# A decoder layer on one core: the first norm rebuilt, the late gates and the seams around the feed-forward reordered

## The chip, the core and the metric

The kernel runs on one core of one Trainium2 chip. It is written for the five engines TensorE (PE), VectorE (DVE), ScalarE (ACT), GpSimd (POOL) and SyncE (SP). Nearly all data transfers (DMAs) are issued on SP, in one list. The metric is the device time of one execution, in microseconds (us); of several executions the median is given.

## What is computed

One layer of a hybrid decoder on 1024 tokens of width 1024, in float32:

```
u = rms_norm(x, g_mix);  z = u @ w_in          # columns shared by all branches
y_nsa = sparse attention (compressed, selected top 8 blocks, window 512), 16 heads
y_rnn = gelu(gate) * rg_lru(causal_conv(z_rnn))
y_x   = cross attention of 4 heads into 256 memory tokens
h = x + (sum of sigmoid(gate_b) * y_b) @ w_o
v = rms_norm(h, g_mlp)
h = h + square(relu(v @ w_up)) @ w_down        # hidden width 4096
out = rms_norm(h, g_final)
```

## The kernel before

**Products.** A float32 product is made of three matmuls of split operands (`mm3`, L80 in the trace): every operand has a hi part, copied by ACT in a narrower type (`split`, L219), and a lo part, the difference, which DVE (L220) or POOL makes. Names ending in h and l, or beginning with whi and wlo, are such parts. Accumulators are PSUM tiles of 128x512: psg, pst, pss, pso.

**Order.** The program is written for a framework that puts each engine's instructions in a list of its own. Every engine runs its list in order, and SP issues transfers in the order of its list; an instruction whose input or buffer is not ready holds back all that stand behind it. A transfer into a buffer of a pool waits until the buffer's last user is done.

**First norm.** `norm_transposed` (L257 to 272) takes 128 tokens: ACT squares and sums (L208, L211), POOL multiplies the second half of the row by the gain (L261), DVE scales (L262, L263), PE transposes eight blocks into two pss tiles, ACT and DVE split them into `uh` and `ul` (L271, L272). The gain lies in SBUF as 128 equal rows. This runs for all eight tiles, and then the projections follow. One weight chunk of 128 columns (`load_split`: raw load wraw, whi, wlo) is used for two halves of 512 tokens: `z_half` is 8 times `mm3`, 24 matmuls, and ends with a copy out of PSUM (zkv for the first four chunks). `weights` splits the next chunk of `plan` while one is in use.

**Early stage and mix.** A `Weave` interleaves several generators on PE by their costs: first the two compressions, one query group, the cross queries and the token values, then attention, recurrence and merge gates up to about 1385 us. In the second one the lo parts of weights are on POOL (L237).

**Late gates and W_o.** For the last two gate chunks (c = 6, 7) and both token halves, PE makes a half, ACT takes tanh (gm, L1005), DVE adds the attention parts (yn2, ymerge), multiplies and adds the recurrence (L1006 to 1008), and SP stores y_d. After each token half `load_wo` loads and splits W_o's half (woh, wol), lo parts on POOL. `out_tile(j)` then loads y_d of row j in four pieces yr, splits them (yh, yl), makes 48 matmuls in two halves, adds the residual, and norms with gmb; `out_forms` transposes the row into the operands B11, B21, B22 and the sums vr.

**Feed-forward.** Both products use seven products of half blocks instead of eight. The up projection has steps (p, s), p = 0 to 15, with s in the order 1, 6, 2, 5, 7, 3, 4 and 12 matmuls each; T1 to T4 are split sums of the normed rows (two pieces each), ura and urb raw weights, uf their split combinations. `finish` combines the products (u, v, c on DVE), squares them, and POOL makes sums as1 to as4. Of each p seven tiles go to `act_d`. The down projection has steps (s, p) in the order s, then p. `fetch` loads one tile araw from act_d and, for s = 1, the first two of four w_down tiles of p (wd, wdf, wdu); `operands` splits them (df) and for s = 1 replaces one weight by a difference (L1289). Four fetches run ahead. The last four steps run together (AT_ONCE).

## Time and profile before

| what | us |
|---|---|
| median of 3 runs | 2174.86 |
| lowest and highest run | 2170.16, 2176.45 |
| profiled execution | 2167.23 |
| its span, first to last instruction | 2165.4 |
| PE busy in it | 2004.4 |
| mean granted clock of PE, share of full | 0.973 |

The profile is of one execution. Busy times are sums over an engine's instructions. A row of a timeline gives the start, the duration, the engine, the source line, the operation with its output and input, how often in a row, and in brackets how long the engine had been idle and what ended that. In a table of windows a matmul that overlaps the next counts until the next begins, so PE cannot be busier than the window. PEclk is the share of its full clock that PE was granted; 1.00 is 2.4 GHz and 0.50 is 1.2 GHz.

### The profile page before, as it was taken

To read this page: it belongs to the slowest core of one execution; us is meant where nothing else is said; L and a number is where in the kernel's file an instruction comes from. 1 tells how busy PE (TensorE), PEld (TensorE's weight loads), DVE (VectorE), ACT (ScalarE), POOL (GpSimd) and SP (SyncE) were. 2 spreads that over 40 slices of the span, in tenths; PEclk is the share of its full clock that TensorE was granted. 3 is DMA by queue.
4 is the path that set the end of the run, shared out by engine and by line. 5 is a ranking of instruction groups with operands and counts; after the bars stand their busy time and mean duration, and the time that the engine had idled before them with its cause. 6 is when DMAs were issued, how large, how long until landed. Compare 5 with 4: busy or idle time off the path is not lost. (4 is left out here: it accounts for less than half of the span.)

```text
span 2165.4 us, 30202 instructions
## 1 busy us (share of the span) xinstructions
PE 2004.4 (93%) x10276; PEld 1673.8 (77%) x10276; DVE 1466.3 (68%) x3215; ACT 1137.8 (53%) x2237; POOL 656.4 (30%) x587
## 2 busy tenths in 40 slices
PE   6988999999998999998999989799899997999997
PEld 5877877888887887777878778677688885888776
DVE  6244386686777777677877767755776675797564
ACT  5234366776667675676677657543322221444353
POOL 2011020333422433243432331412677764010210
PEclk9998999999999999999999999899999999999999
DMA  5466345411441112433123442542444446834433
GB/s 188 139 182 171 105 120 151 130 60 44 107 127 40 59 51 80 129 104 97 56 64 98 137 138 77 184 152 88 146 147 155 156 160 215 305 110 143 141 94 125
DMA packets 160147, 269.36 MB, mean 124 GB/s; under 512 B 19193, under 2 KB 71161, under 8 KB 159993
## 3 DMA queue, kind: packets, MB, share of 16 engines
q1 hardware_dynamic: 159992, 267.44, 39.9%
q8 instruction: 81, 1.33, 0.3%
q14 instruction: 74, 0.60, 0.1%
HBM read 181.39 MB, written 85.98 MB: 123 GB/s over the span
## 5 line engine op out<-in xcount | busy, mean ns | idle before, releaser
L80 PE MATMUL psg<-uh,whi 128*128 128x512 f32 x928 | 381.5, 411 | 10.7 <-DVE qxl L220 7.7
L80 PE MATMUL psg<-uh,wlo 128*128 128x512 f32 x928 | 370.7, 399 | 0.0
L80 PE MATMUL psg<-ul,whi 128*128 128x512 f32 x928 | 369.8, 398 | 0.0
L597 DVE TENSOR_TENSOR pw<-pst,ph 128x512 fp32r<-128x512 f32 (+1 forms) x352 | 217.4, 622 | 71.0 <-ACT ph L596 69.9
L596 ACT ACTIVATE ph<-pst 128x512 fp32r<-128x512 f32 (+1 forms) x352 | 187.3, 538 | 96.0 <-PE pst L84 94.8
L80 PEld LDWEIGHTS psg<-uh,whi 128*128 128x128 f32 x928 | 177.2, 191 | 38.9 <-DVE qxl L220 7.9
L80 PEld LDWEIGHTS psg<-uh,wlo 128*128 128x128 f32 x928 | 177.1, 191 | 38.8 <-DVE wlo L220 1.1
L80 PEld LDWEIGHTS psg<-ul,whi 128*128 128x128 f32 x928 | 178.0, 192 | 25.3 <-issue 0.4
L237 POOL TENSOR_TENSOR wlo<-wraw,whi 128x512 fp32r<-128x512 f32 x100 | 133.7, 1357 | 186.5 <-ACT whi L235 182.6
L80 PE MATMUL pss<-KA,Q 128*128 128x320 f32 (+5 forms) x416 | 145.1, 352 | 8.5 <-DVE sx L774 3.5
L80 PE MATMUL pss<-KB,Q 128*128 128x320 f32 (+5 forms) x416 | 135.3, 328 | 2.0 <-DMA KB<-q_lo 2.0
L80 PE MATMUL pso<-ph,V 128*128 128x256 f32 (+1 forms) x544 | 130.1, 305 | 6.7 <-DVE fold L604 4.7
L778 ACT ACTIVATE E<-E,sx 128x128 f32<-128x128 f32 (+7 forms) x128 | 98.8, 772 | 52.0 <-DVE sx L774 51.4
L80 PE MATMUL pso<-pw,V 128*128 128x256 f32 (+1 forms) x544 | 124.2, 295 | 0.0
L778 ACT ACTIVATE Ew<-Ew,sx 128x640 f32<-128x640 f32 (+4 forms) x128 | 88.5, 692 | 62.3 <-DVE sx L774 61.8
L84 PE MATMUL pst<-ident,E 128*128 128x128 f32 x576 | 94.6, 280 | 23.1 <-DVE pw L597 15.4
L80 PE MATMUL psg<-df 128*128 128x512 f32 x384 | 100.6, 396 | 14.5 <-ACT df L219 13.4
L80 PEld LDWEIGHTS pso<-ph,V 128*128 128x128 f32 x544 | 96.3, 192 | 21.2 <-DVE fold L604 5.0
L220 DVE TENSOR_TENSOR df<-araw,df 128x512 fp32r<-128x512 f32 x112 | 81.2, 729 | 44.1 <-ACT df L219 43.9
L219 ACT ACTIVATE df<-araw 128x512 fp32r<-128x512 f32 x112 | 68.9, 620 | 73.8 <-DMA araw<-act_d 35.5
L80 PE MATMUL pss<-df 128*128 128x512 f32 x432 | 106.2, 389 | 0.7 <-ACT df L219 0.7
L84 PEld LDWEIGHTS pst<-ident,E 128*128 128x128 f32 x576 | 71.6, 143 | 37.0 <-issue 21.6
(405 smaller groups left out, 5043.3 us busy)
## 6 DMA issues: line engine op xcount, KB each, us to landing
wraw<-in_wz SPq DMA_DIRECT2D x59, 512.0 KB
araw<-act_d SPq DMA_DIRECT2D x112, 256.0 KB
act_d<-as SPq DMA_DIRECT2D x64, 256.0 KB
act_d<-sq SPq DMA_DIRECT2D x48, 256.0 KB
yn_d<-parts SPq DMA_DIRECT2D x64, 128.0 KB
ura<-in_w_up SPq DMA_DIRECT2D x16, 512.0 KB
urb<-in_w_up SPq DMA_DIRECT2D x16, 512.0 KB
wdu<-in_w_down SPq DMA_DIRECT2D x32, 256.0 KB
```

The source lines that it names most:

```text
L80: self.tc.nc.tensor.matmul(out, w, x, start=start, stop=stop, skip_group_check=more)
L84: self.tc.nc.tensor.transpose(out, x, ident)
L219: act.activation(hi, src, AF.Copy)
L220: (lo_eng or dve).tensor_tensor(lo, src, hi, OP.subtract)
L237: pool.tensor_tensor(lo[:, x], raw[:, x], hi[:, x], OP.subtract)
L596: act.activation(ph[:rows, :w], pt[:rows, :w], AF.Copy)
L597: dve.tensor_tensor(pw[:rows, :w], pt[:rows, :w], ph[:rows, :w], OP.subtract)
L778: act.activation(E[:, :nw], E[:, :nw], AF.Exp, bias=sx[:, hh:hh + 1], scale=-1.0, accum_out=sx[:, 2 + hh:3 + hh])
```

## The change

- The first norm: the gain is loaded as a column of 128x8 and multiplied in the two splits. DVE scales the x tile in place. Four token tiles are transposed together, feature row by feature row, pss and pst in turn. The order is: norm and split of tokens 0 to 511, norm of the others, first halves of two projection chunks, split of the others, second halves. Raw weights of those chunks are loaded between the x tiles.
- `weights`: the raw load runs two chunks ahead, the split one; the plan already holds five chunks at the start of the early stage. The two compressions are interleaved after 17 and 3 steps.
- Late gates: for the second token half, tanh goes to a DRAM tile tn_d, and the merge follows after row 0 of W_o, in other buffers. W_o's second half gets its lo parts on DVE.
- Last W_o rows: rows 6 and 7 are interleaved by halves; half of T2 and T1 is split before the last half of row 7. `form` takes ten instead of seven early slots.
- Stores of the up projection are collected and issued when step s = 2 of the next p is reached; for the last p they are issued at the fourth down step. The first four down fetches move ahead of the last p's steps, and the differences of w_down are made for p - 3.
- AT_ONCE is 3.

The diff, cut to its core:

```diff
-            uh = actT(F32R, "uh")
-            ul = actT(F32R, "ul")
+            uh, ul = token_halves("uh", "ul")
...
             def weights(src, shape):
-                if not plan:
+                if not plan and not ready:
                     return load_split(src, shape)
-                if not ready:
-                    ready.append(load_split(*plan.pop(0)))
-                w = ready.pop(0)
+                for n in (1, 2):
+                    if len(ready) < n and plan:
+                        what = plan.pop(0)
+                        ready.append([what[1], load_raw(*what), None])
+                for r in ready:
+                    r[2] = r[2] or load_split(None, r[0], raw=r[1])
+                w = ready.pop(0)[2]
                 if plan:
-                    ready.append(load_split(*plan.pop(0)))
+                    what = plan.pop(0)
+                    ready.append([what[1], load_raw(*what), None])
                 return w
...
+                gmix = e0.tile([P, KC], F32, name="gmix")
+                dma(gmix, A["g_mix"])
+                xts, wrs = [], []
                 for j in range(NQ):
+                    if j in (4, 6):
+                        wrs.append(load_raw(*z_weights(KV_CHUNK + len(wrs))))
                     xt = rw("xn") if j < 6 else e0.tile([P, D], F32, name="xn", bufs=2)
                     dma(xt, A["x"][j * P:(j + 1) * P, :])
                     xts.append(xt)
-                    if j == 0:
-                        dma(gmix, A["g_mix"].unsqueeze(0).broadcast_to([P, D]))
-                for j in range(NQ):
-                    xn = e0.tile([P, D], F32, name="xnj", bufs=3)
-                    norm_transposed(xts[j], xn, (gmix[:, :512], gmix[:, 512:]), tok_dst(uh, ul, j))
...
+                def norm_rows(th):
+                    for j in range(4 * th, 4 * th + 4):
+                        x = xts[j]
+                        r = rms_scale(x, e0.tile([P, D], F32, name="xnj", bufs=3))
+                        dve.tensor_scalar(x, x, r, None, OP.mult)
+
+                def feature_rows(th):
+                    for k in range(KC):
+                        pt = (ps_s, ps_t)[k % 2]()
+                        for j in range(4):
+                            pe.transpose(pt[:, j * P:(j + 1) * P], xts[4 * th + j][:, k * P:(k + 1) * P], ident)
+                        h, l = cols(uh, k, th * 512, 512), cols(ul, k, th * 512, 512)
+                        act.activation(h, pt, AF.Copy, scale=gmix[:, k:k + 1])
+                        dve.scalar_tensor_tensor(l, pt, gmix[:, k:k + 1], h, OP.mult, OP.subtract)
...
+                norm_rows(0)
+                feature_rows(0)
+                norm_rows(1)
+                kv0 = [(0, ch, load_split(*z_weights(KV_CHUNK + ch), raw=wrs[ch]), rw("zkv"))
+                       for ch in range(2)]
...
+                for kv, ch, w, zt in kv0:
+                    kv_half(zt, w, 0)
+                feature_rows(1)
+                for kv, ch, w, zt in kv0:
+                    kv_half(zt, w, 1)
+                    kv_store(kv, ch, zt)
...
+                    for x, n in ((a, 17), (b, 3)):
+                        for _ in range(n):
+                            yield next(x)
...
+            def merge_late(t, yn, n2, c, hf):
+                cs = slice(hf * 512, hf * 512 + 512)
+                dma(yn[:, 1, :], yn_d[0][c, :, cs])
+                dma(n2, yn_d[1][c, :, cs])
+                dma(yn[:, 0, :], yr_d[c, :, cs])
+                dve.tensor_tensor(n2, n2, yn[:, 1, :], OP.add)
+                dve.scalar_tensor_tensor(t, t, 1.0, n2, OP.add, OP.mult)
+                dve.tensor_tensor(t, t, yn[:, 0, :], OP.add)
+                dma(y_d[hf][c], t)
...
-                    yn = st("ymerge", F32, (P, 2, 512))
-                    dma(yn[:, 0, :], yr_d[c, :, cs])
-                    dma(yn[:, 1, :], yn_d[0][c, :, cs])
-                    n2 = half2("yn2")
-                    dma(n2, yn_d[1][c, :, cs])
-
                     def use(cs, ps):
                         t = half("gm")
                         act.activation(t, ps, AF.Tanh, scale=0.5)
-                        dve.tensor_tensor(n2, n2, yn[:, 1, :], OP.add)
-                        dve.scalar_tensor_tensor(t, t, 1.0, n2, OP.add, OP.mult)
-                        dve.tensor_tensor(t, t, yn[:, 0, :], OP.add)
-                        dma(y_d[hf][c], t)
+                        if hf:
+                            dma(tn_d[c, :, cs], t)
+                        else:
+                            merge_late(t, st("ymerge", F32, (P, 2, 512)), half2("yn2"), c, hf)
                     for _ in z_half(late[c - 6], hf, use):
                         pass
-                load_wo(hf)
+                load_wo(hf, (pool, dve)[hf])
...
+                if j == 0:
+                    vr.update((n, ox.tile([P, 4, 512], F32, name="vr" + n)) for n in ("11", "21", "12", "22"))
+                    gmb = ox.tile([P, D], F32, name="gmb")
+                    dma(gmb, A["g_mlp"].unsqueeze(0).broadcast_to([P, D]))
+                for nh in range(2):
+                    out_half(row, nh)
+                if j == 0:
+                    for c in (6, 7):
+                        t = spare("gm1")
+                        dma(t, tn_d[c, :, 512:])
+                        merge_late(t, form("ymerge", F32), spare("yn2"), c, 1)
...
+            rows = [out_rows(NQ - 2)]
+            out_half(rows[0], 0)
+            out_forms(NQ - 3, prev)
+            rows.append(out_rows(NQ - 1, form("h7", F32).rearrange("p a b -> p (a b)")))
+            out_half(rows[1], 0)
+            out_half(rows[0], 1)
+            xa = out_norm(NQ - 2, rows[0])
+            first = (("t2", "22"), ("t1", "12"))
+            for n, src in first:
+                t_form(n, src, slice(0, 256))
+            out_half(rows[1], 1)
+            out_forms(NQ - 2, xa)
+            xb = out_norm(NQ - 1, rows[1])
             run(0, 1)
             finish(0, 1)
-            out_forms(NQ - 1, prev)
+            prep(0, 5)
...
+            out_forms(NQ - 1, xb)
             run(0, 2)
-            for n, src in (("t2", "22"), ("t1", "12"), ("t3", "11"), ("t4", "21")):
-                B[n] = vform("T" + n[1], False)
-                for k in (slice(0, 2), slice(2, 4)):
-                    split(B[n][0][:, k, :], B[n][1][:, k, :], vr[src][:, k, :])
+            for n, src in first:
+                t_form(n, src, slice(256, 512))
+            for n, src in (("t3", "11"), ("t4", "21")):
+                t_form(n, src, slice(0, 512))
...
+            stores = []
+
+            def store_acts():
+                while stores:
+                    i, p, t = stores.pop(0)
+                    dma(act_d[i - 1][p], t)
...
-                    for i, t in ((1, a11), (4, a22), (5, s1), (6, s2), (7, s3)):
-                        dma(act_d[i - 1][p], t)
+                    stores.extend((i, p, t) for i, t in ((1, a11), (4, a22), (5, s1), (6, s2), (7, s3)))
...
+                if s == 2:
+                    store_acts()
+                if p == NP - 1 and s == 1:
+                    while n_f < 4:
+                        fetched[dsteps[n_f]] = fetch(*dsteps[n_f], act_tile)
+                        n_f += 1
...
-                    dve.tensor_tensor(w[1], w[1], w[0], OP.subtract)
+                    for x in ((p - 3,) if p < NP - 1 else range(p - 3, NP)):
+                        if x >= 0:
+                            dve.tensor_tensor(wd[x][0][1], wd[x][0][1], wd[x][0][0], OP.subtract)
...
-            AT_ONCE = 4
-            fetched, ready_, banks, keep_ = {}, {}, {}, {}
-            n_f = n_r = 0
-            n = 0
+            AT_ONCE = 3
...
+                if n == 3:
+                    store_acts()
```

The built order, at three places. First ScalarE (ACT) in the first norm. L208 and L213 are the squares of an x tile, L211 and L216 the roots, L219 and L224 hi parts of weights. Before, around the first weights:

```order
L208 ACTIVATE xnj_291,rms_ss_292<-xn_121 128x1024
L211 ACTIVATE rms_r_294<-rms_r_294 128x1
L271 ACTIVATE uh_95<-pss_253 128x4x128
L271 ACTIVATE uh_97<-pss_260 128x4x128
L219 ACTIVATE whi_326<-wraw_324 128x1024
L271 ACTIVATE uh_95<-pss_277 128x4x128
L271 ACTIVATE uh_97<-pss_284 128x4x128
L219 ACTIVATE whi_386<-wraw_384 128x1024
```

After, the same place:

```order
L224 ACTIVATE whi_247<-wraw_115 128x1024
L213 ACTIVATE xnj_215,rms_ss_216<-xn_117 128x1024
L346 ACTIVATE uh_94<-pss_159,gmix_105 128x512
L346 ACTIVATE uh_94<-pst_166,gmix_105 128x512
L346 ACTIVATE uh_94<-pss_173,gmix_105 128x512
L346 ACTIVATE uh_94<-pst_180,gmix_105 128x512
L346 ACTIVATE uh_95<-pss_187,gmix_105 128x512
L346 ACTIVATE uh_95<-pss_201,gmix_105 128x512
L346 ACTIVATE uh_95<-pst_194,gmix_105 128x512
L216 ACTIVATE rms_r_218<-rms_r_218 128x1
L213 ACTIVATE xnj_223,rms_ss_224<-xn_119 128x1024
L346 ACTIVATE uh_95<-pst_208,gmix_105 128x512
```

The first chunk's hi part now stands before all splits of u, each of which covers 512 tokens of one feature row, and the squares of the later tokens stand among them.

Second VectorE (DVE) at the end of the late gates: L1006 to 1008 (now L1048 to 1050) are the merges, yl the lo parts of row 0, wol those of W_o. Before:

```order
L1007 SCALAR_TENSOR_TENSOR gm_14749<-gm_14749,yn2_14722 128x512
L1008 TENSOR_TENSOR gm_14749<-gm_14749,ymerge_14719 128x512
L1006 TENSOR_TENSOR yn2_14778<-yn2_14778,ymerge_14775 128x512
L1007 SCALAR_TENSOR_TENSOR gm_14805<-gm_14805,yn2_14778 128x512
L1008 TENSOR_TENSOR gm_14805<-gm_14805,ymerge_14775 128x512
L1006 TENSOR_TENSOR yn2_14814<-yn2_14814,ymerge_14811 128x512
L1007 SCALAR_TENSOR_TENSOR gm_14841<-gm_14841,yn2_14814 128x512
L220 TENSOR_TENSOR yl_14893<-yr_14894,yh_14892 128x256
L1008 TENSOR_TENSOR gm_14841<-gm_14841,ymerge_14811 128x512
L220 TENSOR_TENSOR yl_14893<-yr_14898,yh_14892 128x256
L220 TENSOR_TENSOR yl_14893<-yr_14902,yh_14892 128x256
L220 TENSOR_TENSOR yl_14893<-yr_14906,yh_14892 128x256
```

After:

```order
L1048 TENSOR_TENSOR yn2_14724<-yn2_14724,ymerge_14723 128x512
L1049 SCALAR_TENSOR_TENSOR gm_14721<-gm_14721,yn2_14724 128x512
L1050 TENSOR_TENSOR gm_14721<-gm_14721,ymerge_14723 128x512
L225 TENSOR_TENSOR yl_14848<-yr_14849,yh_14847 128x256
L225 TENSOR_TENSOR yl_14848<-yr_14853,yh_14847 128x256
L225 TENSOR_TENSOR wol_14811<-woraw_14808,woh_14810 128x1024
L225 TENSOR_TENSOR wol_14811<-woraw_14814,woh_14810 128x1024
L225 TENSOR_TENSOR wol_14821<-woraw_14818,woh_14820 128x1024
L225 TENSOR_TENSOR wol_14821<-woraw_14824,woh_14820 128x1024
L225 TENSOR_TENSOR yl_14848<-yr_14857,yh_14847 128x256
L225 TENSOR_TENSOR yl_14848<-yr_14861,yh_14847 128x256
```

The merges of the second token half have gone from here, and four wol stand between row 0's second and third lo part.

Third SP, where the down projection's first loads are issued. araw are stored activations, sq and as tiles to be stored. Before, at the end of the last p's stores:

```order
L1274 DMA wdu_18391<-in_w_down 128x512
L1189 DMA act_d_85<-sq_18139 128x512
L1274 DMA wdf_18271<-in_w_down 128x512 x2
L1274 DMA wdf_18295<-in_w_down 128x512
L1189 DMA act_d_85<-as1_18157 128x512
L1189 DMA act_d_85<-as2_18158 128x512
L1189 DMA act_d_85<-as3_18159 128x512
L1196 DMA act_d_85<-sq_18182 128x512
L1197 DMA act_d_85<-as4_18184 128x512
L1279 DMA araw_18188<-act_d_85 128x512
L1279 DMA araw_18194<-act_d_85 128x512
L1279 DMA araw_18200<-act_d_85 128x512
```

After, the first araw loads:

```order
L1202 DMA act_d_85<-as2_18009 128x512
L1357 DMA araw_18036<-act_d_85 128x512
L1357 DMA araw_18042<-act_d_85 128x512
L1357 DMA araw_18048<-act_d_85 128x512
L1352 DMA wdf_18050<-in_w_down 128x512 x2
L1357 DMA araw_18053<-act_d_85 128x512
L1352 DMA wdf_18055<-in_w_down 128x512 x2
L1202 DMA act_d_85<-as3_18010 128x512
L1202 DMA act_d_85<-sq_18032 128x512
L1202 DMA act_d_85<-as4_18034 128x512
```

The loads of the first four steps moved from behind the last p's stores to the middle of those of the p before, with their w_down tiles between them.

## Rows read from the trace of the kernel before

**Rows 1.** The page, its first part: busy us, share, instructions of each engine.
```profile
PE 2004.4 (93%) x10276; PEld 1673.8 (77%) x10276; DVE 1466.3 (68%) x3215; ACT 1137.8 (53%) x2237; POOL 656.4 (30%) x587
```

**Rows 2.** Windows: length, then busy us (instructions) of each engine, PEclk, DMA share, GB/s.
```profile
core 0: us, PE busy (x) PEld busy (x) DVE busy (x) ACT busy (x) POOL busy (x), PEclk, DMA share, GB/s
...
0.00:25.00 25.00, 10.14 (x40) 7.55 (x40) 16.23 (x31) 15.33 (x30) 8.53 (x13) 1.00 0.84 308
...
1394.43:1425.00 30.57, 18.05 (x66) 13.74 (x67) 19.21 (x22) 9.81 (x20) 15.04 (x8) 0.78 0.46 153
...
1506.35:1547.00 40.65, 30.07 (x119) 23.29 (x119) 31.59 (x33) 17.29 (x25) 24.84 (x16) 0.92 0.37 122
1818.90:1850.00 31.10, 16.79 (x57) 12.94 (x58) 20.99 (x31) 7.22 (x13) 5.74 (x4) 0.78 0.85 295
1850.00:1875.00 25.00, 25.00 (x112) 20.69 (x111) 14.89 (x24) 10.39 (x18) 0.00 (x0) 1.00 0.94 322
```

**Rows 3.** Timeline, the start: time, duration, engine, line, operation, [idle before]; ACT, DVE, PE.
```profile
4.45 1.06 ACT L208 ACTIVATE xnj<-xn 128x1024 f32<-128x1024 f32 x1 [2.44 <-DMA xn<-in_x]
...
57.37 0.58 ACT L341 ACTIVATE zkv<-psg 128x512 f32<-128x512 f32 x1
...
9.07 1.53 DVE L263 TENSOR_SCALAR xnj<-xn,rms_r 128x512 f32<-128x512 f32 x1
...
12.24 0.47 DVE L263 TENSOR_SCALAR xnj<-xn,rms_r 128x512 f32<-128x512 f32 x1
...
31.66 0.80 PE L80 MATMUL psg<-uh,whi 128*128 128x512 f32 x1
```

**Rows 4.** Timeline, seam 1, in order: PE, DVE, POOL, SP.
```profile
1384.64 0.40 PE L80 MATMUL psg<-uh,whi 128*128 128x512 f32 x1
...
1394.03 0.40 PE L80 MATMUL psg<-uh,wlo 128*128 128x512 f32 x1
...
1405.63 0.76 PE L80 MATMUL psg<-woh,yh 128*128 128x512 f32 x1 [11.20 <-issue]
...
1390.55 0.69 DVE L1007 SCALAR_TENSOR_TENSOR gm<-gm,yn 128x512 f32<-128x512 f32 x1
...
1395.65 2.71 DVE L1007 SCALAR_TENSOR_TENSOR gm<-gm,yn 128x512 f32<-128x512 f32 x1
...
1392.62 10.68 POOL L220 TENSOR_TENSOR wol<-woraw,woh 128x1024 fp32r<-128x1024 f32 x4 [13.24 <-ACT woh L219]
...
1401.14 0.32 SPq L1009 DMA_DIRECT2D y_d<-gm  x1
```

**Rows 5.** Timeline, seam 2: DVE, then PE.
```profile
1511.91 3.61 DVE L220 TENSOR_TENSOR T2l<-vr,T2h 128x1024 fp32r<-128x1024 f32 x2 [1.12 <-ACT T2h L219]
1515.44 2.35 DVE L220 TENSOR_TENSOR T1l<-vr,T1h 128x1024 fp32r<-128x1024 f32 x2
...
1541.01 0.80 PE L80 MATMUL psg<-B21h,uf 128*128 128x512 f32 x1 [4.78 <-ACT p1s L1163]
```

**Rows 6.** Timeline, seam 3: PE, DVE, PE, ACT, SP.
```profile
1822.96 0.50 PE L80 MATMUL pss<-B22h,uf 128*128 128x512 f32 x1 [4.06 <-DVE v L1173]
...
1818.86 0.69 DVE L1289 TENSOR_TENSOR wdf<-wdf 128x512 f32<-128x512 f32 x1 [7.32 <-DMA wdf<-in_w_down]
...
1840.53 3.31 PE L80 MATMUL psg<-df 128*128 128x512 f32 x6 [10.24 <-ACT df L219]
...
1839.32 0.63 ACT L219 ACTIVATE df<-araw 128x512 fp32r<-128x512 f32 x1 [25.18 <-DMA araw<-act_d]
...
1836.52 5.71 SPq L1279 DMA_DIRECT2D araw<-act_d  x8
```

**Rows 7.** Timeline, early stage: ACT, then PE.
```profile
162.74 1.06 ACT L235 ACTIVATE whi<-wraw 128x1024 fp32r<-128x1024 f32 x1 [14.97 <-DMA wraw<-in_wz]
...
165.06 0.80 PE L80 MATMUL psg<-uh,whi 128*128 128x512 f32 x1 [7.70 <-DVE qxl L220]
```

**Rows 8.** The page, its fifth part: one group, the lo parts on POOL.
```profile
L237 POOL TENSOR_TENSOR wlo<-wraw,whi 128x512 fp32r<-128x512 f32 x100 | 133.7, 1357 | 186.5 <-ACT whi L235 182.6
```

More of the change, by code (lines that the diff above doesn't have):

```diff
@@ L146, in body, with token_halves @@
         w4 = w4_stack.enter_context(tc.tile_pool(name="w4", bufs=1))
[L148 to L149 removed]
+        def token_halves(*names):
+            ts = [[[None, None], [None, None]] for _ in names]
+            for th in range(2):
+                for t, n in zip(ts, names):
+                    for kh in range(2):
+                        t[kh][th] = big.tile([P, 4, 512], F32R, name=n, tag="ut", bufs=8)
+            return ts
         def cols(t, k, c0, w):
@@ L1202, in body, with t_form @@
             load_up(0)
-            for j in range(NQ):
-                xt = out_tile(j)
+            def t_form(n, src, js):
+                if n not in B:
+                    B[n] = vform("T" + n[1], False)
+                w = js.stop - js.start
+                for k in ((slice(0, 4),) if w <= 256 else (slice(0, 2), slice(2, 4))):
+                    split(B[n][0][:, k, js], B[n][1][:, k, js], vr[src][:, k, js])
+            for j in range(NQ - 2):
+                row = out_rows(j)
+                if j == 0:
[9 more added lines that the diff above has]
+                        merge_late(t, form("ymerge", F32), spare("yn2"), c, 1)
+                xt = out_norm(j, row)
                 if prev is not None:
@@ L1238, in act_tile @@
                 return ux.tile([P, 512], F32, name=name, tag="a", bufs=8)
-            LEAD = 6
-            finish(0, 2)
-            todo = steps[2:]
-            at = 2
-            for n, (p, s) in enumerate(todo):
-                while at < len(todo) and at <= n + LEAD:
-                    q, u = todo[at]
-                    load_up(q)
-                    prep(q, u)
-                    at += 1
-                    load_up(q + 1)
-                run(p, s)
-                finish(p, s)
             wd = []
@@ L1282, in fetch @@
                 return araw
+            LEAD = 6
+            finish(0, 2)
+            todo = steps[2:]
+            at = 2
+            dsteps = [(s, p) for s in ORDER_P for p in range(NP)]
+            fetched = {}
+            n_f = 0
+            for n, (p, s) in enumerate(todo):
+                if s == 2:
[4 more added lines that the diff above has]
+                        n_f += 1
+                while at < len(todo) and at <= n + LEAD:
+                    q, u = todo[at]
+                    load_up(q)
+                    prep(q, u)
+                    at += 1
+                    load_up(q + 1)
+                run(p, s)
+                finish(p, s)
             def operands(s, p, araw):
```

98 lines of the change are left out of this document (51 added, 47 removed).

## Prediction

> **What bounds the kernel now.** I read the page's busy times first: TensorE (PE) works 93% of the span [rows 1], so the time is PE's work plus the places where PE stops or is given half its clock. A cost on another engine counts only where PE waits for it. The work itself is untouched: the change removes no matrix product, so the most it can bring is the time that PE loses. Then I read the windows for stretches in which PE is far from 25 busy us in 25 [rows 2], and the timelines of all engines there [rows 3 to 6].
>
> At full clock one 128x512 matmul starts 0.229 us after the one before: 42 of them start from 1384.64 to 1394.03 [rows 4]. I call 24 of them a half (5.5 us) and 12 a step (2.75 us). With that price the windows [rows 2] give the loss of each stretch:
> - Start: the first real matmul is at 31.66 us [rows 3]. The fourth half is copied out of PSUM at 57.37 (ScalarE's zkv row).
> - Seam 1, before the W_o rows: 66 matmuls need 15.1 us and take 30.57. Loss 15.5.
> - Seam 2, before the up projection: 119 matmuls, all counted as full ones, need 27.3 us and take 40.65. Loss at least 13.
> - Seam 3, up to down projection: 57 matmuls need 13.1 us and take 31.10. Loss 18.
>
> The change touches all four. Between them PE is close to full, as in the last window of rows 2, and I expect nothing there.
>
> **Part 1, the first norm.** Before, every tile of 128 tokens is multiplied by the gain on POOL and DVE, and the first product waits for eight such tiles, nearly. Removed: 8 POOL multiplies, the 512 KB gain broadcast, and the DVE multiplies by the gain. Added: eight in-place scalings of 128x1024 on DVE. A 128x512 scaling takes 0.47 us, or 1.53 us beside POOL's multiplies [rows 3], so one costs 0.94 to 3.06; since POOL's eight multiplies are gone I take 0.94. The gain now rides in the two splits, which I price as before. The path to the first matmul is then: x0 is there at 4.45; at the window's 308 GB/s a 512 KB tile takes 1.7 us, so x3 is there at about 9.6; square 1.06, root and reciprocal some 0.6, scaling 0.94, transposes and first split some 2 (estimates): first matmul at 14 to 15. The first half runs at the pace of the DVE splits and partly at half clock, to about 22. The second chunk's weight split stands behind the squares of tokens 512 to 1023 on ScalarE, so its half ends near 31. The splits of the later tokens stand behind that half's copy on ScalarE; two more halves end near 44. That is 13 us ahead of 57.4; I take **12**. High end 15, if the second chunk does not wait. Low end 8, if the first 24 matmuls all run at half clock (5.5 us more, of which part is already in the sum).
>
> **Part 2, raw weights two chunks ahead.** The idea fits one wait: ScalarE waits 14.97 us for a raw chunk [rows 7]. In the built order of the SP queue, however, those two raw loads stand behind the same query stores as before, and in the attention and recurrence stage the loads stand where they stood: the scheduler had already moved them as early as the two raw buffers allow. I take **0**. The three interleaved steps of the two compressions move a few matmuls past others: 0 as well, -2 to +2 us.
>
> **Part 3, seam 1.** PE stops after the last gate half and is idle 11.20 us [rows 4]. The chain: the four lo parts of W_o's second half run on POOL (10.68 us for four). Beside them DVE's merge operations take 2.71 us instead of 0.69. So the last y_d store that row 0 needs is issued at 1401.14, and the loads of row 0 stand behind it on SP. After the change these four lo parts are on DVE (four at 1.18 to 1.3, by rows 5 about 1.2: 4.7 us), two of the four merges come after row 0, and the first two loads of row 0 stand ahead of that store. The merge of chunk 7 then ends near 1396.5, and row 0 starts there, 9 us earlier. Three losses remain, since DVE runs its list in order. Row 0's lo parts 4 to 7 stand behind the four W_o splits, so PE waits about 3 us after 12 to 24 matmuls. Row 1's last two loads stand on SP behind the stored late merge, which itself comes behind row 0's end on DVE: about 3 us more. And the clock falls again in such gaps, 1 to 2 us. Of 15.5 I take back **8**; 13 if PE finds other matmuls in the gaps, 4 if each gap also costs a stretch at half clock.
>
> **Part 4, seam 2.** The splits T2, T1, T3, T4 take DVE 3.61 + 3 x 2.35 = 10.7 us [rows 5]. Half of T2 and T1 is now done before the last row's second half, so some 3 us leave the stretch between the last rows and the first products with T4. The 4.78 us stall at 1541.01 hangs on a POOL chain behind the weight load that follows T4; that chain keeps its order and only starts earlier. I take **3**. Zero if the earlier halves just delay the evacuation of the last row, 7 if the small T2 stalls and the stall at 1541 go too.
> The trace shows that DVE and POOL slow each other: T2l took 3.61 beside POOL, T1l 2.35 without. The Trainium skill (GPSIMD Engine Reference, Specifications) says that the two share their SBUF interfaces when a DVE instruction reads two SBUF inputs. That rule speaks against moving the T halves to where POOL makes the sums of the last rows: by it this term would be 2 and the sum 37.
>
> **Part 5, seam 3.** Two stalls. 4.06 us at 1822.96: a sum v stands on DVE behind a wait of 7.32 us for down weights [rows 6]. 10.24 us at 1840.53: the first operand of the down projection waits for its stored activations, whose loads are issued at 1836.52, behind the last stores. The rest of the 18 is half clock. Now the first four loads and their weights stand on SP ahead of the last sums' stores, the first two operands are split during the last up steps, and the weight differences are spread over the steps. The first down product no longer waits. The sum v still stands behind two weight differences whose loads come only a little earlier than before, so I leave up to 3 us of the first stall and its clock. I take **15**, with ends 7 and 18. What is late next: the fifth operand, whose load follows the last as-sums of POOL. Four steps of 2.75 us cover it with about 2 us to spare.
> Three instead of four steps at the very end, and the removed buffers: 0, within 1 us.
>
> **Sum.** 12 + 0 + 8 + 3 + 15 = 38 us. The profiled execution took 2167.23 us (span 2165.4 and 1.8 around it), so it would be 2129. It lies 7.6 us under the median of the runs, 2174.86; I take the 38 from the median: **2137 us**. All high ends (15, 2, 13, 7, 18: 55) give 2120, all low ends (8, -2, 4, 0, 7: 17) 2158.
>
> **Rivals.**
> 1. *Seam 3 is given back to the DMA.* In the first 16 down steps each needs 3 tiles of 256 KB in 2.75 us, 286 GB/s, and 14 delayed stores come on top: 16.3 MB in 44 us is 369 GB/s. The window after the seam moved 322 GB/s at a DMA share of 0.94 [rows 2]: 50.5 us, 6.5 longer. For it: stores now compete with the loads. Against: four steps are fetched ahead while PE still has 19 us of up steps. It would give 2137 + 6.5 = about 2144.
> The Trainium skill (DMA: Bandwidth & Descriptors, Specifications) gives some 358 GB/s as one core's limit to HBM; by that figure the same 16.3 MB take 45.5 us and this rival costs 1.5 us, 2139. No window of rows 2 comes up to it.
> 2. *The start's gain is small.* DVE and ScalarE run in order, and the second chunk's split could hold PE until all eight tiles are scaled. Then only the gain broadcast and the POOL multiplies are saved, about 3 us instead of 12: 2146. For it: that split stands behind the later squares. Against: the first half needs none of them.
> 3. *Slower: the SP queue blocks.* A raw load two chunks ahead takes the buffer that an earlier chunk's split still reads. If such a load stands at the head of SP, everything behind it waits until POOL's lo part is done (100 of them, 1357 ns each, row in [rows 8]), that is 50 chunks. At 1 us of PE wait each, it costs 50: 2137 + 50 = 2187. It decides from 38/50 = 0.76 us a chunk. For it: POOL already spends 182.6 us waiting for the hi parts, so a split that comes late is nothing rare. Against: the SP order is practically the same, and PE's full windows leave no such waits.
> 4. *The two-ahead load does what its words say*, against the built order. The 14.97 us wait goes, and with it at most PE's gap of 7.70 at 165.06 [rows 7]: 2129.
>
> **How the numbers follow.** Forecast 0.58, rival 1 0.14, rival 2 0.14, rival 4 0.05, rival 3 0.04, and 0.05 that several terms fail together and the time stays within 0.3%. A measurement of this kernel tells about 0.3% (6.5 us) from no change. Faster by more: 0.91; within: 0.05; slower: 0.04. Rivals 1, 2 and 4 lie inside the ends of the sum. The upper end of the range is 2158. The lower one is 2114: all high ends, and 6 of the 7.6 us by which the profiled execution lies under the median. Rival 3 and the failures are outside.
>
> **What would show it.** Right: first 128x512 matmul near 15 us and the fourth copy of zkv near 44; no PE gap over 4 us at the W_o rows, DVE merges at 0.69; no PE gap over 3 us where the up projection ends, and the first df split of ScalarE before the last up step. Wrong: the wait of 14.97 us gone; PE gaps with a DMA named in the first 16 down steps (rival 1); raw weight waits of ScalarE in the middle of the kernel (rival 3); T-splits over 3 us each with POOL busy beside them.

## The result

The changed kernel takes 2138.36 us in the median of four runs (2136.38 to 2142.09), the kernel before 2174.13 beside it. The ratio is 0.9839, with a 95% interval of 0.9819 to 0.9859: faster by 35.8 us. The prediction was 2137.0, with a range from 2114 to 2158. Measured once more later, it took 2136.13 beside a median of 2168.45 for the kernel before, ratio 0.9846 (0.9827 to 0.9864): 32.3 us. The profiled execution took 2138.6 us, its span is 2136.8 against 2165.4.

I divided both traces at the same PE instructions. Stage lengths in us (the time from the one instruction to the next):

| stage | before | after | change |
|---|---|---|---|
| start to first matmul of a projection | 31.66 | 14.16 | -17.5 |
| to first memory projection | 50.05 | 54.28 | +4.2 |
| to first key product of attention (early stage) | 191.80 | 189.34 | -2.5 |
| to last late-gate matmul (mix) | 1120.52 | 1129.63 | +9.1 |
| to first W_o matmul of row 0 | 11.60 | 0.23 | -11.4 |
| W_o rows | 96.27 | 99.05 | +2.8 |
| to first matmul with T4 | 26.00 | 26.48 | +0.5 |
| up projection | 302.00 | 300.50 | -1.5 |
| to first down matmul | 10.63 | 0.23 | -10.4 |
| down projection and tail | 324.87 | 322.90 | -2.0 |

These sum to -28.6, the difference of the two spans. The medians differ by 35.8, since the profiled execution of before lay 7 us under its median. The +4.2 belongs to the -17.5 above it (the first matmul now runs before the later tokens are normed), the +2.8 to the -11.4. The one stage that lost with nothing gained beside it, the mix, is taken up in the experiments.

**The page after**, first part, the answer to [rows 1]:

```profile
PE 2000.6 (94%) x10276; PEld 1670.9 (78%) x10276; DVE 1463.2 (68%) x3211; ACT 1135.0 (53%) x2234; POOL 631.6 (30%) x573
```

PE has the same 10276 instructions and 3.8 us less busy time: 24.8 of the 28.6 us were idle time of PE. **Windows of after**, the answer to [rows 2] (start, seam 1, seam 2, seam 3, and twice the down projection behind it), columns as there:

```profile
0.00:25.00 25.00, 14.97 (x78) 12.49 (x79) 15.53 (x36) 21.10 (x42) 1.51 (x7) 1.00 0.78 296
...
1387.80:1418.40 30.60, 26.95 (x110) 21.45 (x109) 18.48 (x30) 12.76 (x27) 6.00 (x4) 0.89 0.70 230
1491.00:1532.00 41.00, 32.79 (x123) 25.00 (x123) 32.79 (x32) 16.02 (x24) 24.56 (x16) 0.88 0.38 119
1803.00:1834.00 31.00, 27.20 (x114) 22.30 (x114) 23.69 (x36) 9.34 (x17) 6.23 (x4) 0.94 0.90 316
1815.00:1840.00 25.00, 25.00 (x112) 20.68 (x111) 17.85 (x27) 10.68 (x19) 5.30 (x4) 1.00 0.95 336
1834.00:1859.00 25.00, 25.00 (x112) 20.68 (x111) 18.41 (x30) 12.36 (x23) 0.00 (x0) 1.00 0.95 339
```

Seam 1 now holds 110 instructions of PE where it held 66, seam 3 114 where it held 57. Seam 2 holds 123 where it held 119: it hardly moved.

**The start**, timeline of after, the answer to [rows 3] (ACT, DVE, PE):

```profile
8.97 0.75 DVE L338 TENSOR_SCALAR xn<-xn,rms_r 128x1024 f32<-128x1024 f32 x1
...
14.16 0.63 PE L80 MATMUL psg<-uh,whi 128*128 128x512 f32 x1
...
22.43 0.64 ACT L359 ACTIVATE zkv<-psg 128x512 f32<-128x512 f32 x1
...
29.15 0.60 ACT L359 ACTIVATE zkv<-psg 128x512 f32<-128x512 f32 x1 [3.58 <-PE psg L80]
...
44.10 0.58 ACT L359 ACTIVATE zkv<-psg 128x512 f32<-128x512 f32 x1
```

The four copies of zkv are the ends of four halves; the fourth stands at 44.10 instead of 57.37.

**Seam 1**, timeline of after, the answer to [rows 4] (PE, DVE, POOL, SP):

```profile
1387.41 0.39 PE L80 MATMUL psg<-uh,wlo 128*128 128x512 f32 x1
1387.64 0.39 PE L80 MATMUL psg<-woh,yh 128*128 128x512 f32 x1
...
1407.09 1.94 PE L84 MATMUL pss<-ident,xres 128*128 128x128 f32 x8 [2.46 <-DVE xres L1131]
1410.02 0.80 PE L80 MATMUL psg<-woh,yh 128*128 128x512 f32 x1 [0.99 <-ACT yh L224]
...
1386.08 2.36 DVE L225 TENSOR_TENSOR wol<-woraw,woh 128x1024 fp32r<-128x1024 f32 x2 [0.52 <-ACT woh L224]
...
1402.63 1.65 DVE L1049 SCALAR_TENSOR_TENSOR gm<-gm,yn 128x512 f32<-128x512 f32 x1
...
1402.12 1.62 POOL L1179 TENSOR_TENSOR urb<-urb 128x512 f32<-128x512 f32 x1
...
1405.58 0.32 SPq L1051 DMA_DIRECT2D y_d<-gm  x1
...
1405.99 0.94 SPq L1108 DMA_DIRECT2D yr<-y_d  x2
```

The 11.20 us gap is gone: row 0 follows the last gate matmul at once. Two W_o lo parts take DVE 2.36 us. What is left is a gap of 2.46 and one of 0.99, 20 us later: the first before the transposes of row 0, whose norm stands on DVE among the late merge, the second at row 1, whose last two loads (yr) are issued right behind the store of that merge (y_d).

**Seam 2**, timeline of after, the answer to [rows 5] (DVE, POOL, PE):

```profile
1474.84 1.32 DVE L225 TENSOR_TENSOR T2l<-vr,T2h 128x1024 fp32r<-128x1024 f32 x1 [1.20 <-ACT T2h L224]
...
1490.93 2.38 DVE L1131 SCALAR_TENSOR_TENSOR xres<-h,rms_r,gmb 128x1024 f32<-128x1024 f32 x1
1493.24 1.76 DVE L225 TENSOR_TENSOR uf<-urb,uf 128x512 fp32r<-128x512 f32 x1
...
1498.47 1.77 DVE L225 TENSOR_TENSOR uf<-ura,uf 128x512 fp32r<-128x512 f32 x1
...
1500.17 2.29 DVE L225 TENSOR_TENSOR T2l<-vr,T2h 128x1024 fp32r<-128x1024 f32 x1
...
1490.97 1.27 POOL L1153 TENSOR_TENSOR vr<-vr,vr 128x512 f32<-128x512 f32 x1 [13.66 <-DVE rms_r L1100]
1492.20 2.26 POOL L1154 TENSOR_TENSOR vr<-vr,vr 128x512 f32<-128x512 f32 x1
...
1526.18 0.50 PE L80 MATMUL psg<-B21h,uf 128*128 128x512 f32 x1 [4.69 <-ACT p1s L1224]
```

The stall of 4.78 us at p1s (the copy of step 1's product, which ScalarE takes out of PSUM) is still 4.69, and these four DVE operations from 1490.93 on, beside POOL, take 1.9 to 2.6 times what they take in the run without POOL beside them, below. T2's first half, moved ahead of the last row, takes 1.32. The same place before, from the last norm on (DVE, then POOL):

```profile
1506.02 1.28 DVE L1076 SCALAR_TENSOR_TENSOR xres<-h,rms_r,gmb 128x1024 f32<-128x1024 f32 x1
...
1507.55 1.45 DVE L220 TENSOR_TENSOR uf<-ura,uf 128x512 fp32r<-128x512 f32 x1 [0.25 <-ACT uf L219]
...
1506.25 2.19 POOL L1098 TENSOR_TENSOR vr<-vr,vr 128x512 f32<-128x512 f32 x1 [8.36 <-DVE vr L1097]
```

**Seam 3**, timeline of after, the answer to [rows 6] (PE, DVE, SP, ACT):

```profile
1806.99 0.80 PE L80 MATMUL pss<-B22h,uf 128*128 128x512 f32 x1 [3.80 <-DVE v L1234]
...
1813.67 0.39 PE L80 MATMUL pss<-T4h,uf 128*128 128x512 f32 x1
1813.90 1.52 PE L80 MATMUL psg<-df 128*128 128x512 f32 x6
...
1803.16 0.69 DVE L1392 TENSOR_TENSOR wdf<-wdf 128x512 f32<-128x512 f32 x1 [1.10 <-DMA wdf<-in_w_down]
...
1806.26 0.68 DVE L1234 TENSOR_TENSOR v<-pss,u 128x512 f32<-128x512 f32 x1
...
1794.86 1.40 SPq L1357 DMA_DIRECT2D araw<-act_d  x3
...
1797.71 0.63 ACT L224 ACTIVATE df<-araw 128x512 fp32r<-128x512 f32 x1 [4.76 <-DMA araw<-act_d]
...
1820.84 0.63 ACT L224 ACTIVATE df<-araw 128x512 fp32r<-128x512 f32 x1 [8.78 <-DMA araw<-act_d]
```

The first activations are loaded at 1794.86 and split at 1797.71, so the first down matmul follows the last up matmul by 0.23 us. The stall on v has only gone from 4.06 to 3.80.

### The profile page after: what moved, and what is told of

The parts are those of the page before. It is cut to its first block, busy times and chain, and to the rows that moved or that the text cites. A ratio compares the mean times of both kernels' runs of the same rounds, so it can differ in the third digit from the quotient of the medians.

```text
span 2136.8 us, 30179 instructions
## 1 busy us (share of the span) xinstructions
PE 2000.6 (94%) x10276; PEld 1670.9 (78%) x10276; DVE 1463.2 (68%) x3211; ACT 1135.0 (53%) x2234; POOL 631.6 (30%) x573
## 4 chain that ended last, share of the span: by engine, by line
PE 60%; DVE 15%; DMA 8%; ACT 6%; issue 6%; POOL 4%; SPq 1%; POOLq 0%; DVEq 0%; ACTq 0%
PE psg L80 29%; PE pss L80 16%; PE pst L80 6%; PE pso L80 5%; PE pst L84 4%; DVE pw L645 2%; DVE W L951 1%; DVE Ew L822 1%; DMA yn<-yn_d 1%; DMA q_hi<-W 1%; DMA wraw<-in_wz 1%; DVE sx L837 1%; DVE E L822 1%; DMA X<-kv_d 1%; DMA q_lo<-W 1%
## 5 line engine op out<-in xcount | busy, mean ns | idle before, releaser
L224 ACT ACTIVATE df<-araw 128x512 fp32r<-128x512 f32 x112 | 69.1, 620 | 68.2 <-DMA araw<-act_d 29.3
```

Source lines behind the costliest of these rows:

```text
L224: act.activation(hi, src, AF.Copy)
```

## The experiments

Each kernel is given with its ratio to the kernel before, timed beside it, whose medians lay between 2168.2 and 2169.1 us.

**The kernel before, once more.** No edit; one profiled run.

> The kernel before once more, for a second trace of it. In its first trace the mix stage, from the first product of queries with keys to the last gate half, took 1120.1 us (273.5 to 1393.6), in the trace of the changed kernel 1129.2 (257.8 to 1387.0). Theory 1 (the first trace was a lucky execution, it lay 7 us under its median): the mix takes 1126 to 1130 here and the span is near 2172. Theory 2 (the change costs the mix 9 us): 1120 again, span near 2166.

It took 2170.36 us, with a span of 2168.6. The same code gave a mix of 1124.42 us where the first trace has 1120.52, between the two theories; the stages around the seams agree within 1.6 us. So a single trace's mix says nothing under some 4 us.

**Part 1 alone**, put on the kernel before.

```diff
-                for j in range(NQ):
-                    xn = e0.tile([P, D], F32, name="xnj", bufs=3)
-                    norm_transposed(xts[j], xn, (gmix[:, :512], gmix[:, 512:]), tok_dst(uh, ul, j))
...
+                norm_rows(0)
+                feature_rows(0)
+                norm_rows(1)
```

> Only the rebuilt first norm, on the kernel before (the gain tile gmb and the sums vr are allocated a row later, which should cost nothing). Theory that the terms add: 13 us off the start stay, 2174 - 13 = 2161. Rival, that later stages are bound by transfers and give the start's gain back: 2168 to 2174, with the mix longer by as much.

2153.56 us, ratio 0.9939 (0.9916 to 0.9962): 14.9 us, and 14.2 in the trace up to the first key product (259.29 against 273.51). Part 1 is worth a little more than the 12 predicted. This kernel also keeps the changed order of the loads around W_o (gmb is loaded a row later, the merges' inputs behind the tanh). Row 0 starts 3.09 us after the last gate matmul, not 11.60, but the rows then take 104.99 instead of 96.27: an earlier start alone brings nothing at seam 1.

**Without part 2.**

```diff
-                for n in (1, 2):
-                    if len(ready) < n and plan:
-                        what = plan.pop(0)
-                        ready.append([what[1], load_raw(*what), None])
...
+                    ready.append(load_split(*plan.pop(0)))
...
-                early.lead(compress_both(), EARLY)
+                early.lead(seq([compress(0, "w_cmp_k1", "w_cmp_k2", "pos_k"),
```

> The changed kernel with the weights one chunk ahead, an empty plan at the start of the early stage and the two compressions one after the other, as before. My theory, that this part is worth 0: 2138, mix 1129. Rival, that the raw loads two ahead cost the mix its 9 us: 2129, mix 1120. Second rival, that the part brings what its words say, the 14.97 us wait: 2142 to 2146.

2136.17 us, ratio 0.9855 (0.9830 to 0.9881): the same time as with it. Part 2 gains nothing that the medians show. In the changed kernel ScalarE's long wait for a raw chunk is still there (ACT), and with it PE's gap:

```profile
146.98 1.06 ACT L245 ACTIVATE whi<-wraw 128x1024 fp32r<-128x1024 f32 x1 [13.50 <-DMA wraw<-in_wz]
...
149.30 0.80 PE L80 MATMUL psg<-uh,whi 128*128 128x512 f32 x1 [6.19 <-DVE qxl L225]
```

**Without part 3** (late merge and W_o lo parts as before).

```diff
-                        if hf:
-                            dma(tn_d[c, :, cs], t)
-                        else:
-                            merge_late(t, st("ymerge", F32, (P, 2, 512)), half2("yn2"), c, hf)
+                        merge_late(t, st("ymerge", F32, (P, 2, 512)), half2("yn2"), c, hf)
...
-                load_wo(hf, (pool, dve)[hf])
+                load_wo(hf, pool)
```

> The changed kernel with the second token half of the late gates merged at once and W_o's second lo parts on POOL, as before. Theory (these two close the first seam, 8.6 us from the last gate half to the end of the W_o rows in the traces): that stretch is 107 to 109 us again instead of 99.3, the time 2138 + 8.6 = 2147. Rival (the earlier allocation order of the loads closes it, not the merge): stretch 99 to 102, time under 2142.

2144.43 us, ratio 0.9899 (0.9872 to 0.9925). Gap and W_o rows take 107.3 us, against 99.3 with part 3: 8.0 us. Merge and lo parts were put back together, so how the 8.0 divide between them is not shown. The timeline (PE, DVE, POOL) has the cause that the prediction gave, four lo parts on POOL and merges of 2.69 beside them:

```profile
1396.50 0.80 PE L80 MATMUL psg<-woh,yl 128*128 128x512 f32 x1 [6.88 <-DVE yl L225]
...
1386.41 2.69 DVE L1049 SCALAR_TENSOR_TENSOR gm<-gm,yn 128x512 f32<-128x512 f32 x1
...
1383.38 10.68 POOL L225 TENSOR_TENSOR wol<-woraw,woh 128x1024 fp32r<-128x1024 f32 x4 [12.93 <-ACT woh L224]
```

**Without part 4** (rows 6 and 7 and the T splits as before).

```diff
-            for j in range(NQ - 2):
+            for j in range(NQ):
...
-            out_half(rows[1], 0)
-            out_half(rows[0], 1)
...
+            for n, src in (("t2", "22"), ("t1", "12"), ("t3", "11"), ("t4", "21")):
```

> The changed kernel with rows 6 and 7 one after the other and T1 to T4 split whole after the last row, as before. My term was 3 us; the traces show the stretch from the last W_o matmul to the first product with T4 at 26.5 us against 26.0 and 27.6 in two traces of before. Theory now (the earlier halves lie beside POOL and cost what they save): rows plus that stretch 125.8 us within 1, time 2138. Rival (the term of 3 is there, hidden by something else): 2141.

2137.18 us, ratio 0.9864 (0.9839 to 0.9889). W_o rows and stretch to T4 take 124.96 us, with part 4 125.53 and 124.36 in two traces. Part 4 is worth 0, not 3.

**Seam 2 without POOL.** The sums vr of rows 6 and 7 and three activation sums (as1 to as3) of p = 0 go from POOL to DVE.

```diff
-                        pool.tensor_tensor(vr["21"][:, :, js], vr["21"][:, :, js], t2, OP.subtract)
+                        eng = dve if j >= 6 else pool
+                        eng.tensor_tensor(vr["21"][:, :, js], vr["21"][:, :, js], t2, OP.subtract)
...
-                    pool.tensor_tensor(s1, a21, a22, OP.add)
+                    eng = dve if p == 0 else pool
+                    eng.tensor_tensor(s1, a21, a22, OP.add)
```

> The changed kernel with POOL's sums for rows 6 and 7 (four) and the as-sums of p = 0 (three) moved to DVE, 7 x 0.69 = 4.8 us more work there. Theory (DVE is slowed beside POOL: 2.29 us for one T2l piece of 1.18, 2.38 for a scaling of 1.28, 1.75 to 1.78 for uf splits of 0.68): pieces at their lone times, the first products with T4 1 to 2 us earlier, the 4.69 us gap at p1s down to 2 to 3, time 2138 - 3 = 2135. Rival (the seam hangs on the weight load after the splits, not on DVE's speed): gaps as they are or longer by the added work, 2138 to 2142.

2132.74 us, ratio 0.9845 (0.9821 to 0.9869). Its timeline (DVE, PE) shows the same operations as in seam 2 of after, at their own price:

```profile
1488.34 1.28 DVE L1131 SCALAR_TENSOR_TENSOR xres<-h,rms_r,gmb 128x1024 f32<-128x1024 f32 x1
1489.53 0.69 DVE L225 TENSOR_TENSOR uf<-urb,uf 128x512 fp32r<-128x512 f32 x1
...
1495.37 1.23 DVE L225 TENSOR_TENSOR T2l<-vr,T2h 128x1024 fp32r<-128x1024 f32 x1
...
1516.78 0.50 PE L80 MATMUL psg<-B21h,uf 128*128 128x512 f32 x1 [1.52 <-ACT p1s L1225]
...
1529.23 0.50 PE L80 MATMUL pss<-B22h,uf 128*128 128x512 f32 x1 [3.98 <-DVE v L1235]
```

2.38, 1.76 and 2.29 became 1.28, 0.69 and 1.23, the stretch to T4 fell from 26.48 to 23.98, the p1s stall from 4.69 to 1.52. A new wait of 3.98 on v came 12 us later. Over all traces with part 4 the stretch is 25.4 to 26.6 us in the six with POOL's sums and 23.9 to 24.0 in the four without them, so POOL beside DVE costs it 1.4 to 2.7 us, even with the sums' own time then on DVE. The kernel without part 4 was not run with these sums on DVE; that they cost just part 4's gain is therefore not shown. For the whole time the intervals do not part this kernel from the changed one.

**Without part 5** (stores at once, no early fetch, differences at s = 1).

```diff
+                    store_acts()
...
-                if s == 2:
-                    store_acts()
-                if p == NP - 1 and s == 1:
-                    while n_f < 4:
...
-                    for x in ((p - 3,) if p < NP - 1 else range(p - 3, NP)):
...
+                    dve.tensor_tensor(w[1], w[1], w[0], OP.subtract)
```

> The changed kernel with the up projection's stores issued at once, the down projection's first fetches after the last up step, and the weight differences made in the step that needs them. Theory (this part alone closes the third seam): 2138 + 13 = 2151, PE gaps of about 4 and 10 us back. Rival (the seam closes because other parts moved the queue): under 2143.

2147.66 us, ratio 0.9911 (0.9883 to 0.9940), 11.5 us more than the kernel without part 2, timed beside it. The three edits were put back together, so their shares are not shown. Its timeline (PE, ACT, SP) is that of before again:

```profile
1820.37 3.31 PE L80 MATMUL psg<-df 128*128 128x512 f32 x6 [9.65 <-ACT df L224]
...
1819.17 0.63 ACT L224 ACTIVATE df<-araw 128x512 fp32r<-128x512 f32 x1 [23.98 <-DMA araw<-act_d]
...
1816.36 5.71 SPq L1359 DMA_DIRECT2D araw<-act_d  x8
```

**The w_down differences on POOL.** A test of the 3.80 us stall that part 5 left.

```diff
-                            dve.tensor_tensor(wd[x][0][1], wd[x][0][1], wd[x][0][0], OP.subtract)
+                            pool.tensor_tensor(wd[x][0][1], wd[x][0][1], wd[x][0][0], OP.subtract)
```

> The changed kernel with the w_down differences on POOL instead of DVE. Theory (the 3.80 us gap that is left at the third seam comes from the sum v, which stands on DVE behind two such differences that wait for their loads): gap 2.5 or less, time 2138 - 1 to -3. Rival (the gap comes from the activation load whose split stands before v as well, landed at 1803.8): gap 3 or more, no change.

2133.68 us, ratio 0.9841 (0.9820 to 0.9862). The stall is gone (PE, then POOL), so it was DVE's queue of differences:

```profile
1802.85 0.50 PE L80 MATMUL pss<-B22h,uf 128*128 128x512 f32 x1 [0.36 <-DVE v L1234]
...
1800.14 1.51 POOL L1392 TENSOR_TENSOR wdf<-wdf 128x512 f32<-128x512 f32 x1 [4.85 <-DMA wdf<-in_w_down]
```

The up projection is 4.8 us shorter; the down projection is 1.7 longer (324.7), but two kernels without this edit have 324.4 as well. Against the changed kernel's 0.9839 and 0.9846 the time is not told apart.

**The changed kernel again.** No edit, as the measure for the next two.

> The changed kernel once more, beside the two below. If the mix stage differs between executions of one kernel (1120.5 and 1124.4 us in two traces of before, 1121 to 1130 in eight kernels whose mix was not touched but for the load order), it is between 1120 and 1130 here too, and all other stages are within 1 us of the first trace: start to first key product 257.8, gates to rows' end 99.3, up stage 300.5, down stage 310.5. Rival (the change itself makes the mix 9 us longer): 1129 or more again.

2136.13 us, ratio 0.9846 (0.9827 to 0.9864). The mix is 1128.85 us, as long as in the first trace of this kernel, which fits either statement on it within 0.2 us; the stretch to T4 is 1.1 us shorter, the other stages agree within 0.5.

**Both edits**, of seam 2 without POOL and of the differences on POOL.

```diff
+                        eng = dve if j >= 6 else pool
...
+                    eng = dve if p == 0 else pool
...
+                            pool.tensor_tensor(wd[x][0][1], wd[x][0][1], wd[x][0][0], OP.subtract)
```

> The changed kernel with POOL's sums for rows 6 and 7 and the as-sums of p = 0 on DVE, and the w_down differences on POOL: both edits at once. If they add (3.8 and 3 us in the traces): 7 us under the changed kernel of this call. If the second is given back in the down stage (312.3 against 310.5 us): 4 to 5.

2131.02 us, ratio 0.9828 (0.9807 to 0.9850). Stretch to T4 and up projection take 318.4 us, against 326.1 (25.35 + 300.73) in the changed kernel timed beside it. Of these 7.7 the medians show 5.1, inside the intervals.

**Both edits, the activation sums left on POOL.** The second of the three lines above is left out.

> As the one before, but the as-sums of p = 0 stay on POOL. In the trace with them on DVE the 4.69 us gap at p1s fell to 1.52 while a new one of 3.98 came at a sum v just behind. If the two only trade places, this kernel is as fast as the one before within 1 us; if moving the as-sums is what helps, it is 2 us slower.

2132.41 us, ratio 0.9832 (0.9816 to 0.9848), the two stages 321.6 us. So of the 7.7 us some 3 hang on the activation sums. No form of the two edits is shown to beat the changed kernel; the two timed beside it lie 5.1 and 3.7 us under it, and by their ratios the two single edits do not lie under it at all.

**Both edits, without part 2**, whose diff stands above. The mix was 1120.5 to 1124.4 us in the four traces without part 2 and 1125.3 to 1130.1 in nine with it.

> The kernel both_fixes (2131.0) without the raw weights two chunks ahead: the plan is filled ahead as before, the compressions stand together as before. Theory that part 2 costs the first norm's mix some 5 us (the stretch from the first key product to the last gate matmul was 1120.5 to 1124.4 in four traces without it, 1125.3 to 1130.1 in those with it): that stretch is 1124.5 or shorter, and the median about 2126, ratio to before about 0.980. Rival, that the stretch's length is only the spread between executions: median about 2131, ratio 0.983 as both_fixes, the stretch anywhere between 1120 and 1130. The opposite, that part 2 does what its words say: 2133 or longer.

2129.16 us, ratio 0.9823 (0.9797 to 0.9848). The mix is 1121.68, as the first theory said and the rival allows; the time is 1.9 us under that with part 2, between the 5 of the one and the 0 of the other. The windows of the mix, with part 2 (both edits) and without:

```profile
259.00:1389.00 1130.00, 1058.02 (x5840) 887.77 (x5839) 837.46 (x2271) 753.33 (x1525) 351.53 (x381) 0.98 0.32 95
```

```profile
263.00:1384.00 1121.00, 1055.26 (x5836) 885.83 (x5835) 833.66 (x2271) 753.29 (x1526) 353.72 (x382) 0.98 0.32 97
```

PE is idle 72.0 us in the first and 65.7 in the second. Over all traces the idle time of the mix is 65.4 to 67.1 us in five without part 2 and 66.2 to 72.0, mean 69.8, in nine with it; the early stage is 190.4 to 194.2 without and 188.6 to 190.8 with. Both stages together are 1312.0 to 1315.9 us without and 1315.1 to 1320.7 with part 2, on average 3.1 us longer. What PE waits for in the mix names the place, again with part 2 (both edits) and without, us in total, times, longest:

```profile
PE pso L80 <- ACT parts L871: 8.5, 7, 2.6
```

```profile
PE pso L80 <- ACT parts L856: 5.5, 5, 1.6
```

PE's next product into an accumulator of the attention (pso) waits until ScalarE has copied an earlier one out of PSUM (parts). This wait takes 7.5 to 9.2 us in the nine traces with part 2 and 4.9 to 5.6 in the five without; a second one, on a sum cS of POOL, takes 2.2 to 2.3 against 0.8 to 0.9. These two are some 4 us. Why ScalarE and POOL come later to them stays open, and so does what part 2 does to the whole time, since both pairs of medians differ by less than their intervals.

## Why the prediction was right

- **Part 1: 12, measured 13.3 to 15.7.** The steps held: first matmul at 14.16 (14 to 15), first half copied at 22.43 (22), second at 29.15 (31), fourth at 44.10 (44). At the fourth half the gain is 13.3 us, at the first key product 15.7, of which some 2 lie in the early stage and may be its spread. The in-place scaling was cheaper than priced, 0.75 us for 128x1024 and not 0.94. Rival 2, 3 us, is refuted: part 1 alone brought 14.9.
- **Part 2: 0, measured 0 by the medians.** The 14.97 us wait is 13.50 and PE's gap 6.19 instead of 7.70. Rival 4, that the wait goes, is refuted, and rival 3 at its 50 us too: the kernel is 35.8 us faster, and without part 2 it takes the same time. The traces lean to a loss of some 3 us, with PE's longer waits in the mix, a stage for which I had expected nothing because the loads stand there where they stood.
- **Part 3: 8, measured 8.6 (8.0 by its removal).** The total was right, its parts less so. Row 0 starts at once and waits 0.20 us where I had 3 for the W_o lo parts on DVE. The other loss is there: gaps of 2.46 and 0.99 us before the second part of row 1, whose loads do stand behind the late merge's store, and half clock behind it (granted 0.50 from 1410.0 to 1413.6), some eight matmuls 0.43 us apart instead of 0.229, 1.6 us. The sign "merges at 0.69" holds for the first token half; a multiplication of the late merge takes 1.65 us beside a POOL operation of 1.62.
- **Part 4: 3, measured 0.** This step failed, as a size at the low end that I had named, and the reason named there (a later copy of the last row) is not what the trace shows. The term counted what leaves the stretch, and that part is right: the moved halves take DVE 1.32 us (T2) and 1.22 (T1). It did not count what comes in. The last norm takes 2.38 us for 1.28 before, and three lo parts of up weights (uf, 1.76, 0.68 and 1.77) stand ahead of T4 where before one stood at 1.45: 3.9 us more, of which 1.4 is the price of two more lo parts at 0.69 and the rest POOL's sums vr beside them. One of the two is new there by the change itself, which prepares the weights of step 5 behind the last row. From the last row's residual sum to the last lo part of T4 DVE needs 19.5 us in both traces. T2's second half was slow before as well: its two halves are 1.32 and 2.29, together the 3.61 of [rows 5]. I used that 3.61 against 2.35 for a discount of 1 us, in a sentence beside the sum, instead of asking which operations would newly stand beside POOL. So the sign that I had named for this failure, T splits over 3 us each, did not come, and the failure came all the same.
The Trainium skill (GPSIMD Engine Reference, Specifications) has the two engines share their SBUF interfaces for DVE instructions with two SBUF inputs. These rows agree with it, and its side of the sum, 2, was the nearer one; it was still above the measured 0.
- **Part 5: 15, measured 12.4 (11.5 by its removal).** The 10.24 us gap went whole, with 2.0 in the down projection. The 1.5 us by which the up projection is shorter are not counted: in the second trace of the kernel before it takes 300.40, as long as after. What was too large is what I took back of the first stall: I left 3 us of it and its half clock. It cost 3.80 us, against the sign that no gap over 3 is left there, and then 1.4 at half clock (granted 0.52 from 1807 to 1810), seven matmuls of B22 that take 3.04 us instead of 1.60. The wait for the w_down load did shrink, from 7.32 to 1.10 us, but v then stood behind five other DVE operations from 1803.16 to 1806.26. A wait in an in-order list was replaced by a queue.
Rival 1 is refuted: PE is busy 25.00 of 25 us in both windows behind the seam, at 336 and 339 GB/s and a DMA share of 0.95, above the 322 that I had taken for the limit. The fifth operand, split from 1820.84, is needed at 1824.78: the cover that I named was enough.
The Trainium skill (DMA: Bandwidth & Descriptors, Specifications) has 358 GB/s as a core's limit to HBM. The two windows of 25 us stay under it, but the ten us from 1830 to 1840 moved 389 GB/s (counted by the start of each transfer, at a share of 1.05), so no run here shows it as a ceiling for so short a stretch.
- **The sum.** 38 predicted. By the terms it is 13.3 to 15.7, 0, 8.6, 0 and 12.4, together 34 to 37; the medians gave 35.8 at first and 32.3 later (2168.45 less 2136.13), and the terms less the 3 us that the traces lean to for part 2 are 31 to 34. Too little on part 1 made up for too much on parts 4 and 5. That the forecast came within 1.4 us is luck in one more way: the median from which I took the 38, 2174.86, lies some 6 us above the four later ones of the same kernel (2168.2 to 2169.1), and 38 is some 6 too much. From the later medians the same 38 would give 2130 to 2131.

## What to carry to other kernels

Before you move DVE work into a gap, look at what POOL does in that gap, price the work by a row in which both run, and count what the reordering brings into the gap as well as what leaves it. When a load is brought forward to end a wait in an engine's in-order list, count what stands in that list between the wait and the instruction that matters: that queue is the next wait. Price a seam from the idle time of the engine that bounds it, cut the traces at the same instructions afterwards, and trace the same kernel twice before you explain a stage of 1100 us by a few.

## What was not expected of the hardware

- In the rows of seam 2 DVE lost nearly the same beside POOL whatever the size: 128x512 lo parts 0.69 to 1.76 us, 128x1024 ones 1.23 to 2.29, the norm 1.28 to 2.38, 1.06 to 1.10 us each, beside sums that take POOL 1.27 alone. Beside POOL's W_o lo parts of some 2.7 us each the merges went from 0.69 to 2.69, 2.0 us. POOL loses too: its sum took 1.27 and 2.26 us, and before, the norm took 1.28 beside a sum of 2.19. The prediction had one such pair.
- Two executions of the kernel before differ by 3.9 us in the mix (1120.52 and 1124.42) with the same instructions, and places of low clock differ: the stretch from 820 to 830 us has a granted clock of 1.00 in one and 0.83 in the other.
